# A two-layer hybrid attention trunk: polynomial logarithm, a fourth raw weight buffer, other copies for queries and keys, and a shifted order

## The chip, the core and the metric

The kernel runs on one core of a Trainium2 chip. The metric is the device time of one execution, in microseconds. A core has TensorE (PE, with its weight loads shown apart as PEld), VectorE (DVE), ScalarE (ACT), GpSimd (POOL) and SyncE (SP, which here only issues transfers). The profile shows each engine's instructions with the line of the source that issued them.

## The reference

A trunk of two layers on x of 256 x 1024. Each layer normalises x, projects it with one matrix to all that the mixers need, runs three causal mixers of eight heads of 64 (MoBA, DSA, FoX), multiplies each by its SiLU gate, projects each back, merges the three by sigmoid gates and adds the output projection to x:

```
h = rms_norm(x, gain);  proj = h @ w_in          # 1024 -> 9296 columns
oa = moba(rope(qa), rope(ka), va) * silu(ga)
ob = dsa(rope(qb), rope(kb), vb, rope(q_idx), rope(k_idx), w_idx) * silu(gb)
log_f = log_sigmoid(f_logit + f_bias)            # 256 x 8
oc = fox(qc, kc, vc, log_f) * silu(gc)           # logits += cumsum(log_f)[t] - cumsum(log_f)[s]
y = stack([oa, ob, oc]) @ w_branch               # 512 -> 1024 each
x = x + sum(sigmoid(merge) * y) @ w_out
```

With 256 tokens the MoBA mixer is plain causal attention. DSA scores all keys with eight index heads, `sum_h w[t,h] * relu(q_idx . k_idx)`, and each query keeps its 64 best.

## The kernel before

**Split products.** All matrix products are made from two parts of each operand, a high one (what is left of an fp32 number after rounding to the type fp32r) and a low one (the rest): high x high, low x high and high x low. So a weight piece is loaded into a `raw` buffer by SP, ACT writes its high part `wh` (L374), DVE writes `wl = raw - wh` (L378), and PE runs the 24 matmuls of a unit (L419, 128 x 256 results, into one of three PSUM banks `proj`). Six `wh` and six `wl` ring slots and three `raw` buffers are cycled.

**Units.** The projection goes in units of 128 columns: the index key (`kwf`, with the DSA weights and FoX logits beside it), four index queries, then for each mixer four pairs of heads with a query, a key and a gate unit, merge gates, and the units of w_branch and w_out. A unit's result is taken from PSUM by DVE and ACT.

- Rope (index, MoBA and DSA queries and keys): DVE shuffles rows into `rsh` (L468), POOL multiplies it (L469), DVE makes `rr` (L470), POOL adds them (L471). There are two buffers of each.
- `write_q` (a query): ACT writes the high part `qh` (L405 or, with a scale, L409) and DVE the low part `qy` (L406, L410). Since PE contracts over 128 rows and a head has 64, ACT then packs by three half-height copies (L591): `qx` gets head 0's high rows and its low rows, and `qy` head 1's high rows above its low ones.
- `write_bd` (a key): ACT copies the rows of each head into the high tile `bd..h` twice (L744 from the source, L746 from itself to the other half), four half-height copies, and DVE writes the low rows `bd..l` (L748).
- Scores: three matmuls (L604, L606 twice) for 128 queries, three for the other 128, into the two PSUM banks `s`.
- Index heads: ACT takes relu out of the two banks (L818, 256 columns; L819, 512 columns) into `tmp`, DVE adds it up, weighted, in `isc` (L827, L829). Then eight rounds of MAX and MATCH_REPLACE (L849, L850) find the 64 best.
- Attention: DVE adds the mask and takes row maxima (L665, into `e` and `st`), ACT exponentials (L669), DVE reciprocals (L673), ACT or DVE the normalisation (L677 or L680), PE transposes (L692) into the two PSUM banks `t`, ACT and DVE split the result (L695, L697), PE multiplies by the values (L708 to L711) into the one PSUM bank `o`.
- Logarithm of the forget gates: `fz` holds six small tiles of 128 x 16. ACT takes an exponential (L777) and Ln (L778), DVE corrects the result for small arguments in nine steps (L782 to L790), and PE forms the cumulative sum (L796, L797). An instruction `ACT_TABLE_LOAD` stands ahead of Ln (L778) and ahead of the first tanh after it (L863).
- Merge: the tanh of a gate goes to `acc` (L863) or `mth`; later DVE multiplies and adds the branches (L897, L899; POOL can do the add, L900).

**What sets the order.** The order of every engine is fixed ahead by a list scheduler in the program (`Plan.run`). Each operation has one or more engines, costs, the buffers it uses and a key, which is mostly the number of its unit. The scheduler goes through a model of the time; the engine that can start first takes, of the operations that could start by then, the one with the smallest key. A tile is given to an operation when one of its kind is free, so the number of buffers changes the order too.

Of the kernel before, what the change touches and what calls it, by code (L numbers as in the profile page):

```python
# [9 lines left out]
F32 = mybir.dt.float32  # L10
F32R = mybir.dt.float32r
AF = mybir.ActivationFunctionType
ALU = mybir.AluOpType

L = 2
S = 256
# [13 lines left out]
C_ID, C_UT, C_MASK, C_ROPE, C_END = 0, 128, 256, 512, 1024  # L30
SWAP = list(range(8, 16)) + list(range(0, 8)) + list(range(16, 32))

R_RING = 6
R_RAW = 3
# [17 lines left out]
def shape_constants():  # L52
# [18 lines left out]
    return c  # L71

# [23 lines left out]
class Plan:  # L96
# [8 lines left out]
    def op(self, ways, reads, writes, key, lag=0.0, name="", touch=()):  # L105
# [20 lines left out]
        o.n, o.out, o.need, o.end = len(self.ops), [], 0, None  # L126
        for d in o.deps:
            if d is not o:
                d.out.append(o)
                o.need += 1  # L130
# [113 lines left out]
def hybrid_trunk(ctx, tc, x, norm_gain, w_in, forget_bias, w_branch, w_out, final_gain, consts, out):  # L244
# [15 lines left out]
    def T(b):  # L260
        return b.slot[1]
# [83 lines left out]
    for nm, n, cols, dt in (("rsh", 2, S, F32), ("rr", 2, S, F32),  # L345
# [238 lines left out]
    def write_q(src, n_ps, key, scale=None, name="q"):  # L584
# [5 lines left out]
        for t, o, a, b, i in ((q[1], up, q[0], up, 0), (q[1], dn, q[2], up, 1), (q[2], up, q[0], dn, None)):  # L590
            act(lambda t=t, o=o, a=a, b=b: ACT.activation(T(t)[o], T(a)[b].bitcast(F32), AF.Copy), S, False, [a],  # L591
                [q[2]] if i is None else [kx[i]], key, name, touch=[t], half=True)
# [142 lines left out]
    def write_bd(src, b, toks, key, ps, shared=False):  # L735

        up, dn = slice(0, 64), slice(64, 128)
        for h, o in enumerate((up, dn)):
# [4 lines left out]
            if not (shared and h):  # L743
                act(lambda hi=hi, s=s: ACT.activation(hi(), s(), AF.Copy), S, ps, [src], [toks[g][0]], key, "bd", touch=[b], half=True)  # L744
# [5 lines left out]

# [7 lines left out]
    def wf_cols(l, key):  # L758
# [17 lines left out]
        def ln():  # L776
            ACT.activation(e, na, AF.Exp)  # L777
            ACT.activation(u, e, AF.Ln, bias=1.0)  # L778
        act(ln, 0, False, [], [k_lf], key, "ln", 1540.0)
        act(lambda: None, 0, False, [k_lf], [], key - 1, "table", 1190.0)  # L780

        for f in (lambda: DVE.tensor_scalar(c, e, 1.0, None, op0=ALU.add),  # L782
                  lambda: DVE.tensor_scalar(na, c, 1.0, None, op0=ALU.is_equal),
                  lambda: DVE.tensor_scalar(c, c, -1.0, 5e-8, op0=ALU.add, op1=ALU.max),
                  lambda: DVE.reciprocal(c, c),
                  lambda: DVE.tensor_tensor(c, c, e, op=ALU.mult),
                  lambda: DVE.tensor_tensor(u, u, c, op=ALU.mult),
                  lambda: DVE.tensor_tensor(na, na, e, op=ALU.mult),
# [328 lines left out]
```

## Time and profile before

| what | value |
|---|---|
| time, median of 3 runs (lowest to highest) | 618.05 us (617.97 to 618.89) |
| time of the profiled execution | 618.74 us |
| its span | 616.9 us |
| PE busy | 606.5 us (98%) |
| DVE busy | 534.5 us (87%) |
| ACT busy | 451.7 us (73%) |
| POOL busy | 95.0 us (15%) |
| granted PE clock, mean | 0.997 |
| moved by DMA | 107.32 MB, mean 174 GB/s |

The span runs from the first to the last thing that the profile shows; 618.74 - 616.9 = 1.84 us of the execution lie around it. A row of a timeline gives the start (us from the span's start), the duration, engine, line, operation and tiles, and in brackets how long the engine had been idle and who released it. Instructions of an engine overlap a little, so what one costs in a row of them is the distance from its start to the next one's. The chain of waits follows the end back to its causes and gives for each piece only the time that counts.

### The profile page before, as it was taken

To read this page: it belongs to the slowest core of one execution; us is meant where nothing else is said; L and a number is where in the kernel's file an instruction comes from. 1 tells how busy PE (TensorE), PEld (TensorE's weight loads), DVE (VectorE), ACT (ScalarE), POOL (GpSimd) and SP (SyncE) were. 2 spreads that over 40 slices of the span, in tenths; PEclk is the share of its full clock that TensorE was granted. 3 is DMA by queue.
4 is the path that set the end of the run, shared out by engine and by line. 5 is a ranking of instruction groups with operands and counts; after the bars stand their busy time and mean duration, and the time that the engine had idled before them with its cause. 6 is when DMAs were issued, how large, how long until landed. Compare 5 with 4: busy or idle time off the path is not lost.

```text
span 616.9 us, 12615 instructions
## 1 busy us (share of the span) xinstructions
PE 606.5 (98%) x4804; PEld 581.1 (94%) x4804; DVE 534.5 (87%) x1322; ACT 451.7 (73%) x948; POOL 95.0 (15%) x101
## 2 busy tenths in 40 slices
PE   8999999999999999999999999999999999999995
PEld 6899999999998999999889999998999989999985
DVE  7899999985998889988588999998678988999773
ACT  5788398876996778775587866997688766987541
POOL 1251242000000233200006305300000013220001
PEclk9999999999999999999999999999999999999998
DMA  8962765655554563575555639455637365453711
GB/s 283 304 195 90 226 171 191 200 171 172 171 173 136 180 197 99 175 237 173 158 170 174 204 114 276 141 170 185 209 103 231 112 201 157 155 169 122 257 35 69
DMA packets 96156, 107.32 MB, mean 174 GB/s; under 512 B 4576, under 2 KB 84832, under 8 KB 96096
## 3 DMA queue, kind: packets, MB, share of 16 engines
q1 hardware_dynamic: 95808, 106.13, 54.7%
q8 instruction: 37, 0.61, 0.4%
q10 hardware_dynamic: 288, 0.39, 0.2%
q14 instruction: 23, 0.19, 0.1%
HBM read 103.37 MB, written 1.05 MB: 169 GB/s over the span
## 4 chain that ended last, share of the span: by engine, by line
PE 78%; DVE 13%; ACT 4%; issue 2%; DMA 1%; POOL 1%; SPq 0%; POOLq 0%; DVEq 0%; ACTq 0%
PE proj L419 68%; DVE wl L378 5%; PE t L692 3%; DVE isc L850 2%; PE proj L996 1%; PE s L604 1%; PE s L606 1%; DVE t L849 1%; DMA x<-in_x_dram 1%; DVE isc L829 1%; DVE rsh L468 1%; ACT wh L374 1%; PE o L708 1%; PE o L711 1%; DVE rr L470 1%
## 5 line engine op out<-in xcount | busy, mean ns | idle before, releaser
L419 PE MATMUL proj<-hTh,wh 128*128 128x256 f32 (+1 forms) x1040 | 270.1, 278 | 0.0
L419 PE MATMUL proj<-hTl,wh 128*128 128x256 f32 (+1 forms) x1040 | 269.7, 277 | 0.0
L378 DVE TENSOR_TENSOR wl<-raw,wh 128x1024 fp32r<-128x1024 f32 (+1 forms) x190 | 235.5, 1248 | 38.3 <-ACT wh L374 37.7
L374 ACT ACTIVATE wh<-raw 128x1024 fp32r<-128x1024 f32 (+1 forms) x190 | 199.0, 1053 | 51.1 <-PE proj L419 41.3
L419 PE MATMUL proj<-hTh,wl 128*128 128x256 f32 (+1 forms) x1040 | 234.0, 278 | 0.0
L419 PEld LDWEIGHTS proj<-hTh,wh 128*128 128x128 f32 (+1 forms) x1040 | 194.7, 187 | 0.2
L419 PEld LDWEIGHTS proj<-hTl,wh 128*128 128x128 f32 (+1 forms) x1040 | 194.6, 187 | 0.3
L419 PEld LDWEIGHTS proj<-hTh,wl 128*128 128x128 f32 (+1 forms) x1040 | 175.6, 187 | 0.0
L469 POOL TENSOR_TENSOR rsh<-rsh,cst 128x256 f32<-128x256 f32 (+1 forms) x42 | 35.6, 849 | 351.9 <-DVE rsh L468 351.7
L471 POOL TENSOR_TENSOR rr<-rr,rsh 128x256 f32<-128x256 f32 (+1 forms) x42 | 51.1, 1220 | 8.2 <-DVE rr L470 5.4
L669 ACT ACTIVATE e<-e,st 128x128 f32<-128x128 f32 x96 | 42.7, 446 | 6.9 <-DVE st L665 6.6
L419 PE MATMUL proj<-wh,v 128*128 128x512 f32 (+1 forms) x144 | 35.5, 368 | 0.0
L419 PE MATMUL proj<-og0l,wh 128*128 128x256 f32 x128 | 33.9, 277 | 0.0
L419 PE MATMUL proj<-og0h,wh 128*128 128x256 f32 x128 | 32.4, 278 | 0.0
L419 PE MATMUL proj<-wh,hTh 128*128 128x512 f32 x80 | 32.4, 405 | 0.0
L419 PE MATMUL proj<-wh,hTl 128*128 128x512 f32 x80 | 31.5, 393 | 0.0
L419 PEld LDWEIGHTS proj<-wh,v 128*128 128x128 f32 x144 | 25.2, 188 | 4.7
L419 PE MATMUL proj<-og0h,wl 128*128 128x256 f32 x128 | 28.6, 277 | 0.0
L697 DVE TENSOR_TENSOR ptl<-t,pth 128x384 fp32r<-128x384 f32 x48 | 24.9, 551 | 0.6 <-ACT pth L695 0.6
L419 PE MATMUL proj<-wl,hTh 128*128 128x512 f32 x80 | 24.9, 392 | 0.0
L419 PEld LDWEIGHTS proj<-og0h,wh 128*128 128x128 f32 x128 | 24.0, 188 | 0.0
L419 PEld LDWEIGHTS proj<-og0l,wh 128*128 128x128 f32 x128 | 24.0, 188 | 0.0
(194 smaller groups left out, 1046.1 us busy)
## 6 DMA issues: line engine op xcount, KB each, us to landing
raw<-in_w_in_dram SPq DMA_DIRECT2D x74, 1024.0 KB, 5.3
raw<-in_w_branch_dram SPq DMA_DIRECT2D x24, 512.0 KB, 3.5
raw<-in_w_out_dram SPq DMA_DIRECT2D x8, 1024.0 KB, 6.9
tmp<-wf SPq DMA_DIRECT2D x16, 128.0 KB, 5.2
raw<-in_w_in_dram SPq DMA_DIRECT2D x3, 512.0 KB, 7.9
x<-in_x_dram SPq DMA_DIRECT2D x4, 256.0 KB, 5.1
raw<-in_w_in_dram SPq DMA_DIRECT2D x2, 320.0 KB, 6.0
out_dram<-tmp SPq DMA_DIRECT2D x2, 320.0 KB, 2.5
```

The source lines that it names most:

```text
L374: ACT.activation(p[0].v, sel(c.v), AF.Copy)
L378: DVE.tensor_tensor(p[1].v, sel(c.v), p[0].v.bitcast(F32), op=ALU.subtract)
L419: PE.matmul(o(), a(), b(), start=first and i == 0, stop=last and i == n - 1)
L468: dve(lambda: DVE.stream_shuffle(T(sh)[:np_], a(), SWAP), S, [ps], [sh], key, "rope")
L469: gps(lambda: POOL.tensor_tensor(T(sh)[:np_], T(sh)[:np_], s[:np_], op=ALU.mult), S, [k_rope], [sh], key, "rope")
L470: dve(lambda: DVE.tensor_tensor(T(r)[:np_], a(), c[:np_], op=ALU.mult), S, [ps, k_rope], [r], key, "rope")
L471: gps(lambda: POOL.tensor_tensor(T(r)[:np_], T(r)[:np_], T(sh)[:np_], op=ALU.add), S, [sh], [r], key, "rope")
L604: PE.matmul(o.rearrange("p (h c) -> p h c", h=2), qh[:, sl], kl[:, :, :n], start=True, stop=False)
L669: act(lambda t=t, a=a, n=n, e=e, st=st: ACT.activation(T(e)[:, a:a + n], T(e)[:, a:a + n], AF.Exp, bias=T(st)[:, t:t + 1], scale=-1.0, acc ...
L692: PE.transpose(T(ps)[:, i * 128:(i + 1) * 128], T(es[h])[:, i * 128:(i + 1) * 128], ident)
L697: dve(lambda h=h, src=src: DVE.tensor_tensor(T(pl)[:, h], src(), T(ph)[:, h].bitcast(F32), op=ALU.subtract), 384, [ps, kp[h][0]], [kp[h][1 ...
L850: dve(lambda o=o, t8=t8: DVE.match_replace(o, T(t8), o, TAKEN), n, [t8], [k_isc[i]], key + r * step, "top8")
```

## The change

It does four things.

1. The logarithm is computed without Ln. After the exponential e, DVE makes s = e / (2 + e) and sums an odd polynomial in s (`ATANH`), ten steps in place of nine. Ln and the operation "table" that was scheduled ahead of it are gone; so are the four `ACT_TABLE_LOAD` at L778 and L863.
2. There are four `raw` buffers for three, and four each of `rsh` and `rr` for two. The space comes from `dynamic_dma_scratch_size=1024`.
3. `write_q` makes `qx` by one full-height copy straight from the source, which puts head 0's high rows in place, and a half copy over its lower half; the copy into `qy` stays. `write_bd` of a key makes the high tile by one full-height copy of 512 columns and two half copies for four half copies. The index key (`shared`) keeps its copies.
4. A table `SHIFT` adds a number between -9 and 2 to the keys of 229 operations, by their running number.

The diff, with one line of the table:

```diff
-R_RAW = 3
+R_RAW = 4
...
+ATANH = (2.0, 0.666663146821, 0.400249102795, 0.279606027472, 0.281783350867)
...
+SHIFT = {
+    115: 1, 142: -6.5, 144: -0.5, 145: -7, 146: -1, 148: -3, 150: -5, 160: 2, 172: 2, 173: -6, 174: -1, 192: -4,
...
         o.n, o.out, o.need, o.end = len(self.ops), [], 0, None
+        o.key += SHIFT.get(o.n, 0.0)
...
-    for nm, n, cols, dt in (("rsh", 2, S, F32), ("rr", 2, S, F32),
+    for nm, n, cols, dt in (("rsh", 4, S, F32), ("rr", 4, S, F32),
...
-        for t, o, a, b, i in ((q[1], up, q[0], up, 0), (q[1], dn, q[2], up, 1), (q[2], up, q[0], dn, None)):
-            act(lambda t=t, o=o, a=a, b=b: ACT.activation(T(t)[o], T(a)[b].bitcast(F32), AF.Copy), S, False, [a],
-                [q[2]] if i is None else [kx[i]], key, name, touch=[t], half=True)
+        if scale is None:
+            act(lambda: ACT.activation(T(q[1]), src[0](), AF.Copy), S, n_ps, [src[1]], kx, key, name, touch=[q[1]])
+        else:
+            act(lambda: ACT.activation(T(q[1]), src[0](), AF.Copy, scale=scale), S, n_ps, [src[1]], kx, key, name, touch=[q[1]])
+        act(lambda: ACT.activation(T(q[1])[dn], T(q[2])[up].bitcast(F32), AF.Copy), S, False, [q[2]], [kx[1]], key, name,
+            touch=[q[1]], half=True)
+        act(lambda: ACT.activation(T(q[2])[up], T(q[0])[dn].bitcast(F32), AF.Copy), S, False, [q[0]], [q[2]], key, name, half=True)
...
+        if not shared:
+            act(lambda: ACT.activation(T(b)[0], T(src)[:, :S].unsqueeze(1).to_broadcast([128, 2, S]), AF.Copy), 2 * S, ps, [src],
+                [toks[0][0], toks[0][1], toks[1][0], toks[1][1]], key, "bd", touch=[b])
...
-                act(lambda hi=hi, s=s: ACT.activation(hi(), s(), AF.Copy), S, ps, [src], [toks[g][0]], key, "bd", touch=[b], half=True)
...
-        def ln():
-            ACT.activation(e, na, AF.Exp)
-            ACT.activation(u, e, AF.Ln, bias=1.0)
-        act(ln, 0, False, [], [k_lf], key, "ln", 1540.0)
-        act(lambda: None, 0, False, [k_lf], [], key - 1, "table", 1190.0)
+        act(lambda: ACT.activation(e, na, AF.Exp), 16, False, [], [k_lf], key, "lf")
+
+        s, s2, q = na, c, u
+        for f in (lambda: DVE.tensor_scalar(s2, e, 2.0, None, op0=ALU.add),
+                  lambda: DVE.reciprocal(s2, s2),
+                  lambda: DVE.tensor_tensor(s, e, s2, op=ALU.mult),
+                  lambda: DVE.tensor_tensor(s2, s, s, op=ALU.mult),
+                  lambda: DVE.tensor_scalar(q, s2, ATANH[4], ATANH[3], op0=ALU.mult, op1=ALU.add),
+                  lambda: DVE.tensor_tensor(q, q, s2, op=ALU.mult),
+                  lambda: DVE.scalar_tensor_tensor(q, q, ATANH[2], s2, op0=ALU.add, op1=ALU.mult),
+                  lambda: DVE.scalar_tensor_tensor(q, q, ATANH[1], s2, op0=ALU.add, op1=ALU.mult),
+                  lambda: DVE.scalar_tensor_tensor(q, q, ATANH[0], s, op0=ALU.add, op1=ALU.mult),
+                  lambda: DVE.scalar_tensor_tensor(lf, z, 0.0, q, op0=ALU.min, op1=ALU.subtract)):
...
-    nc = _bacc.Bacc("TRN2", target_bir_lowering=False, num_devices=1)
+    nc = _bacc.Bacc("TRN2", target_bir_lowering=False, num_devices=1, dynamic_dma_scratch_size=1024)
```

As the order counts instructions, PE stays at 4145 rows (a row can stand for several equal matmuls) with the same matmuls, and its projections keep their order: only the score, transpose, value and sum matmuls move among them. ACT goes from 846 instructions to 811, DVE from 1250 to 1260, POOL from 106 to 103 (four adds L899 to DVE, a gate product to POOL). On DVE there are also six normalisations more that ACT had before, and one less. The first rows that differ stand at about 28 us of the profile before on ACT and DVE and at about 40 us on PE; from about 575 us on the order of the three is the same again. After the change L374 is L401, L405 and L409 are L432 and L436, L406 and L410 are L433 and L437, L419 is L446, L468 is L495, L591 is L618 to L623, L665 is L696, L796 is L829, L818 and L819 are L851 and L852, L863 is L896.

The order at three places follows, at the second of them on two engines; the digits behind a name tell buffers apart, and they differ between the kernels.

ACT in the index stage of the first layer, before, from the large relu of one pair of index heads (L819, `tmp` from the second score bank) to the next one and past it:

```order
L819 ACTIVATE tmp_108<-s_163 128x512
L591 ACTIVATE qy_87<-qh_81 64x256
L591 ACTIVATE qx_85<-qh_82 64x256
L591 ACTIVATE qx_85<-qy_88 64x256
L591 ACTIVATE qx_83<-qh_80 64x256
L591 ACTIVATE qy_88<-qh_82 64x256
L591 ACTIVATE qx_83<-qy_86 64x256
L863 ACTIVATE acc<-proj_161 128x256
L374 ACTIVATE wh_67<-raw_120 128x1024
L818 ACTIVATE tmp_108<-s_162 128x256
L591 ACTIVATE qy_86<-qh_80 64x256
L819 ACTIVATE tmp_108<-s_163 128x512
```

The same place after, from the large relu (L852) to the next:

```order
L852 ACTIVATE tmp_108<-s_168 128x512
L896 ACTIVATE acc<-proj_166 128x256
L401 ACTIVATE wh_67<-raw_118 128x1024
L621 ACTIVATE qx_83<-qy_86 64x256
L851 ACTIVATE tmp_108<-s_167 128x256
L623 ACTIVATE qy_86<-qh_80 64x256
L852 ACTIVATE tmp_108<-s_168 128x512
```

Six half copies, of three index queries, stood ahead of acc and the weight split (L374) between the two relus, and one behind them; now one half copy stands behind acc and wh and one between the small and the large relu. The other copies of those queries are fewer, or stand ahead of the first relu.

DVE where the last steps of the logarithm (`fz`) are done in the first layer, before:

```order
L788 TENSOR_TENSOR fz<-fz 128x16
L849 MAX t_147<-isc 128x8
L789 TENSOR_TENSOR fz<-fz 128x16
L849 MAX t_148<-isc 128x8
L790 SCALAR_TENSOR_TENSOR fz<-fz 128x16
L850 MATCH_REPLACE isc<-t_147,isc 128x128
L850 MATCH_REPLACE isc<-t_148,isc 128x256
L633 SCALAR_TENSOR_TENSOR g_127<-th_125,proj_160 128x256
L378 TENSOR_TENSOR wl_75<-raw_118,wh_68 128x1024
L800 COPY csum<-t_165 128x16
L803 COPY wf<-t_165 128x256
L801 TENSOR_SCALAR ncs<-t_165 128x16
```

After:

```order
L819 TENSOR_TENSOR fz<-fz 128x16
L883 MATCH_REPLACE isc<-t_153,isc 128x256
L820 SCALAR_TENSOR_TENSOR fz<-fz 128x16
L405 TENSOR_TENSOR wl_70<-raw_119,wh_63 128x1024
L821 SCALAR_TENSOR_TENSOR fz<-fz 128x16
L405 TENSOR_TENSOR wl_71<-raw_120,wh_64 128x1024
L822 SCALAR_TENSOR_TENSOR fz<-fz 128x16
L664 SCALAR_TENSOR_TENSOR g_133<-th_131,proj_165 128x256
L823 SCALAR_TENSOR_TENSOR fz<-fz 128x16
L405 TENSOR_TENSOR wl_72<-raw_120,wh_65 128x1024
L882 MAX t_154<-isc 128x8
L833 COPY csum<-t_170 128x16
```

The steps on `fz` were set between the rounds of the search; now three `wl`, two gate products `g` and a search round more stand ahead of the last of them, and what reads the cumulative sum (csum) comes later by as much.

PE at that cumulative sum, before:

```order
L419 MATMUL proj_161<-hTh,wh_67 128x256
L419 MATMUL proj_161<-hTl,wh_67 128x256
L796 MATMUL t_165<-fz,cst 128x16
L797 MATMUL t_165<-fz,ones 128x8
L419 MATMUL proj_161<-hTh,wl_74 128x256
L419 MATMUL proj_161<-hTh,wh_67 128x256
```

After, with the six rows ahead of it:

```order
L446 MATMUL proj_164<-hTh,wh_68 128x256
L446 MATMUL proj_164<-hTh,wl_75 128x256 x2
L446 MATMUL proj_164<-hTl,wh_68 128x256
L446 MATMUL proj_164<-hTh,wl_75 128x256
L829 MATMUL t_170<-fz,cst 128x16
L830 MATMUL t_170<-fz,ones 128x8
L446 MATMUL proj_166<-hTh,wh_63 128x256
L446 MATMUL proj_166<-hTl,wh_63 128x256
```

The sum stood behind the first six matmuls of the unit in the third `proj` bank; now it stands behind 42 projection matmuls more, at the start of the unit after the next.

DVE at the row maxima of the first attention pair to be scored (`e` and `st` from the banks `s`), before, all four of them, with the low part of a query (`qy`) between:

```order
L378 TENSOR_TENSOR wl_72<-raw_119,wh_65 128x1024
L665 ISA e_131,st_135<-s_162,cst 128x128
L665 ISA st_135 128x1
L665 ISA e_131,st_135<-s_163,cst 128x256
L665 ISA st_135 128x1
L665 ISA e_132,st_136<-s_162,cst 128x128
L665 ISA st_136 128x1
L410 SCALAR_TENSOR_TENSOR qy_86<-rr_124,qh_80 128x256
L665 ISA e_132,st_136<-s_163,cst 128x256
L665 ISA st_136 128x1
L378 TENSOR_TENSOR wl_73<-raw_120,wh_66 128x1024
```

After:

```order
L437 SCALAR_TENSOR_TENSOR qy_86<-rr_127,qh_80 128x256
L495 STREAM_SHUFFLE rsh_124<-proj_165 128x256
L497 TENSOR_TENSOR rr_128<-proj_165,cst 128x256
L696 ISA e_136,st_140<-s_167,cst 128x128
L696 ISA st_140 128x1
L696 ISA e_137,st_141<-s_167,cst 128x128
L696 ISA st_141 128x1
L696 ISA e_136,st_140<-s_168,cst 128x256
L696 ISA st_140 128x1
L696 ISA e_137,st_141<-s_168,cst 128x256
L696 ISA st_141 128x1
L704 RECIPROCAL st_140<-st_140 128x1
```

The copy qy went from between the maxima to ahead of them, and the order of the four is now: both of the smaller bank, then both of the larger one.

More of the change, by code (lines that the diff above doesn't have):

```diff
@@ L71, in shape_constants @@
     return c
+SHIFT = {
[21 rows of a table added]
+}
 CUR = [""]
@@ L737, in write_bd @@
         up, dn = slice(0, 64), slice(64, 128)
+        if not shared:
+            act(lambda: ACT.activation(T(b)[0], T(src)[:, :S].unsqueeze(1).to_broadcast([128, 2, S]), AF.Copy), 2 * S, ps, [src],
+                [toks[0][0], toks[0][1], toks[1][0], toks[1][1]], key, "bd", touch=[b])
+        else:
+            act(lambda: ACT.activation(T(b)[0][up, 0], T(src)[up, :S], AF.Copy), S, ps, [src], [toks[0][0]], key, "bd", touch=[b],
+                half=True)
         for h, o in enumerate((up, dn)):
@@ L774, in wf_cols @@
         dve(pre, 0, [ps, k_fb], [k_lf], key, "lf", 300.0)
-        def ln():
-            ACT.activation(e, na, AF.Exp)
-            ACT.activation(u, e, AF.Ln, bias=1.0)
-        act(ln, 0, False, [], [k_lf], key, "ln", 1540.0)
-        act(lambda: None, 0, False, [k_lf], [], key - 1, "table", 1190.0)
[L782 to L788, printed above, removed]
-                  lambda: DVE.tensor_tensor(u, u, na, op=ALU.add),
-                  lambda: DVE.scalar_tensor_tensor(lf, z, 0.0, u, op0=ALU.min, op1=ALU.subtract)):
+        act(lambda: ACT.activation(e, na, AF.Exp), 16, False, [], [k_lf], key, "lf")
[10 more added lines that the diff above has]
+                  lambda: DVE.scalar_tensor_tensor(lf, z, 0.0, q, op0=ALU.min, op1=ALU.subtract)):
             dve(f, 0, [], [k_lf], key + 10, "lf", 100.0, port=True)
```

20 rows, old and new, of the table SHIFT are left out of this document.

## The prediction

> **What bounds the kernel now.** I read the page first. Its chain of work that ended last names the engine that sets the end:
>
> ```profile
> span 616.9 us, 12615 instructions
> ...
> PE 78%; DVE 13%; ACT 4%; issue 2%; DMA 1%; POOL 1%; SPq 0%; POOLq 0%; DVEq 0%; ACTq 0%
> ```
>
> The end hangs on PE for 78% of the span and on DVE for 13%. The order gives PE the same 4145 rows, with the same matmuls, before and after the change. So the time can fall only where PE stands still, and the second view is the waits of PE's weight loads, from 20 us to the end (columns: who waits, for whom, us in total, times, longest):
>
> ```profile
> PEld s L604 <- ACT tmp L819: 1.0, 3, 0.5
> PEld t L796 <- DVE fz L790: 0.8, 2, 0.6
> PEld t L692 <- ACT e L677: 0.3, 1, 0.3
> PEld o L708 <- ACT bd0h L744: 0.3, 1, 0.3
> PEld s L604 <- DVE st L665: 0.2, 1, 0.2
> ```
>
> These five rows are all that PE waits for after 20 us: eight waits, 1.0 + 0.8 + 0.3 + 0.3 + 0.2 = 2.6 us. Ahead of that, and in the last stage (from 575 us), the rows of PE, DVE and ACT stand in the same order in both kernels, so the waits there are taken as unchanged. **The most that this change can take out is about 2.6 us, 0.42% of the span.**
>
> Third, busy time by stage, to see who has room where these waits lie (first layer's index stage, its selection stage, and the second layer's selection stage; columns: stretch, its length, busy PE, PEld, DVE, ACT, POOL, then clock, DMA share, GB/s):
>
> ```profile
> 31.00:60.00 29.00, 28.63 (x246) 28.24 (x245) 26.91 (x71) 25.34 (x48) 10.65 (x11) 1.00 0.48 150
> 60.00:88.00 28.00, 27.91 (x240) 27.48 (x239) 27.88 (x86) 17.12 (x35) 9.91 (x8) 1.00 0.68 201
> 360.00:388.00 28.00, 27.54 (x237) 27.03 (x236) 27.88 (x86) 17.03 (x36) 8.99 (x8) 1.00 0.74 216
> ```
>
> ACT is busy 25.34 of 29 us in the index stage and has 11 us free in the selection stage, where DVE has nothing free: 27.88 of 28 us, in both layers.
>
> **Edit 1: the copies for queries and keys (ACT).** What a half-height copy takes, as a group of ACT's (x count: shortest/median/longest ns), and then two pieces of the chain of waits (start, us that count, what) for the next prices:
>
> ```profile
> L591 ACT ACTIVATE qx<-qh x32: 397/417/422, 36.5 to 541.8; 64x256 fp32r<-64x256 f32 x32
> ```
>
> ```profile
> 43.01 0.30 ACT qh L405
> 43.31 0.50 ACT tmp L819
> ```
>
> A query unit had three half-height copies, 3 x 0.42 = 1.26 us; it gets one full-height copy, priced by the qh row of the same size at 0.30, and two halves, 0.84: 1.14 us, so 0.12 saved, 32 times: 3.8 us. A key unit had four halves of the same 64x256, 1.68 us; it gets one full copy of 512 columns, by the 512-column relu 0.50, and two halves: 1.34, so 0.34 saved, 24 times: 8.2 us. That is 12 us. The trace of before has neither full copy in that place; if they took 0.42, as much as a half, and 0.57, as the longest relu below, the savings would be 0 and 0.27 x 24 = 6.5 us. ACT has room in each of the stages above, so nearly all of these 6.5 to 12 us lies beside PE's work and counts nothing. It counts where a half copy stands ahead of something PE waits for. That place is this, on ACT and then on PE:
>
> ```profile
> 46.48 0.38 ACT L863 ACTIVATE acc<-proj 128x256 f32<-128x256 f32 x1
> 46.76 1.05 ACT L374 ACTIVATE wh<-raw 128x1024 fp32r<-128x1024 f32 x1
> 47.71 0.37 ACT L818 ACTIVATE tmp<-s 128x256 f32<-128x256 f32 x1
> 48.11 0.41 ACT L591 ACTIVATE qy<-qh 64x256 fp32r<-64x256 f32 x1
> 48.43 0.57 ACT L819 ACTIVATE tmp<-s 128x512 f32<-128x512 f32 x1
> ```
>
> ```profile
> 49.06 0.50 PE L604 MATMUL s<-bd0l,qh 128*128 128x512 f32 x1 [0.37 <-ACT tmp L819]
> ```
>
> PE needs the second score bank, which relu L819 empties at 49.00; the one before it ended at 43.81 (43.31 + 0.50). Between them ACT ran six half copies, acc, wh, the small relu and another half copy: 5.2 us. In the new order only acc, wh, a half copy, the small relu and a half copy stand between the same two relus. By starts in these rows that is acc 0.28 (46.48 to 46.76), wh 0.95, half 0.44, small relu 0.40, half 0.32 and the relu's 0.57: 2.96 us. The bank comes free 2.2 us earlier, PE asks for it 0.5 us earlier than it got it, and in the new order that third score group also stands six projection matmuls (0.7 us) further up: about 1 us to spare. The same holds in the second layer. Taken: the 1.0 us of the first row goes, all of it. In the FoX units the full copy reads the projection's own bank, so 16 times a bank is read 0.30 us longer or less; no row of PE waits for a projection bank, so this counts zero (if that cover were gone: up to 16 x 0.30 = 4.8 us).
>
> **Edit 2: the logarithm.** The table loads, as the group at L778, and one of those at L863 with what follows it:
>
> ```profile
> L778 ACT ACT_TABLE_LOAD  x2: 1283/1283/1283, 28.8 to 327.9; - x2
> ```
>
> ```profile
> 40.11 1.28 ACT L863 ACT_TABLE_LOAD   x1
> 41.41 0.38 ACT L863 ACTIVATE acc<-proj 128x256 f32<-128x256 f32 x1
> ```
>
> The load at L778 and the one back at L863 stand once in each layer: 4 x 1.28 = 5.1 us of ACT go. The Trainium skill ("ScalarE: Activation LUTs", section "What ACT_TABLE_LOAD costs") adds a drain of about 1.38 us to each load, by which the four would be worth 10.6 us. The trace shows no such drain: the load from 40.11 to 41.39 is followed by acc at 41.41. Either way PE does not wait on these loads, so they count zero by themselves; their cover is the weights already split ahead. The ten polynomial steps on DVE replace nine, one more small step in each layer. What decides is when the last is done, for PE's cumulative sum (L796) waits for it. DVE there, first the chain of waits, with a stretch of 42 projection matmuls as PE's price, then the engine's own rows:
>
> ```profile
> 60.77 0.07 DVE fz L790
> 60.85 0.66 DVE isc L850 x3
> 61.50 0.33 DVE g L633
> 61.83 1.14 DVE wl L378
> ...
> 93.98 4.77 PE proj L419 x42
> ```
>
> ```profile
> 46.85 0.18 DVE L786 TENSOR_TENSOR fz<-fz 128x16 f32<-128x16 f32 x1
> 47.06 0.18 DVE L787 TENSOR_TENSOR fz<-fz 128x16 f32<-128x16 f32 x1
> 47.85 1.23 DVE L378 TENSOR_TENSOR wl<-raw,wh 128x1024 fp32r<-128x1024 f32 x1 [0.61 <-ACT wh L374]
> ```
>
> The order moves the cumulative sum behind 42 more projection matmuls: 4.77 us later. It also puts more of DVE's work ahead of the last log step: three wl (3 x 1.14), two g (2 x 0.33), one search pair (0.66) and one step net (0.07), together 4.8 us. The two shifts cancel; but PE now arrives earlier by the waits gone ahead of it: first layer 0.5 (score bank) + 0.2 (its own old wait) = 0.7 us, second layer 0.5 + 0.6 = 1.1 us. So if DVE is as idle as before, waits of 0.7 and 1.1 us stand there, 1.8 us where 0.8 stood. What DVE gets back: the six log steps that ran one behind the other at 0.21 us each (46.85 to 47.06) are now set between other work, where one costs 0.07 (60.77 to 60.85): some 6 x 0.14 = 0.8 us; and the 0.61 us that it stood idle for a wh which was queued behind half copies. That is up to 1.4 us in a layer, more than 1.1. Taken: 0.2 us in each layer, between 0 and the 1.8 for both. So 0.8 goes and 0.4 comes.
>
> **Edit 3: four raw buffers, four for the rope.** What ACT's weight split waits for, over the whole run (us, times):
>
> ```profile
>   PE proj L419: 41.3, 44
>   DMA raw<-in_w_in_dram: 6.1, 5
> ```
>
> The split waits 44 times for PE to give up a ring slot and five times, 6.1 us, for a load; no row of PE above waits for a weight. A raw buffer more lets loads start earlier into time that PE does not lack: taken at zero, with the split ring as cover. The smaller scratch for dynamic DMA touches no load here, as SP and ACT issue them all. The rope buffers matter by what they allow to overlap; that is the second rival.
>
> **Edit 4: the shifted order.** It takes the copy qy (L410) out from between the row maxima of the first attention pair:
>
> ```profile
> 85.44 0.41 DVE L410 SCALAR_TENSOR_TENSOR qy<-rr,qh 128x256 fp32r<-128x256 f32 x1
> 85.77 0.41 DVE L665 CUSTOM_DVE_ANT_0 e<-s,cst 128x256 f32<-128x256 f32 x1
> ```
>
> The copy costs 0.33 (start to start) and the last maximum ended at 86.18, just when PE wanted the bank. Without it the bank is free 0.33 us earlier, which covers the wait of 0.2. The other two single waits (0.3 and 0.3) are at places where the order also moved rows; they may go or move. Four adds of the merge (L899) go from POOL to DVE, at 0.33 by the copy's row, 1.3 us in all: zero, as no row of PE waits in the merge stage. Moved groups can also meet new waits. Before, six of the eight waits, 1.8 us, lay at the some hundred attention groups of PE, the other two at the sums. I take new ones at 0.4 us, a quarter of that; the bounds are 0 and 1.8.
>
> **The sum.** 2.6 out, 0.4 in at the cumulative sums, 0.4 in elsewhere: 1.8 us less. The profiled execution (618.74 us, its span 616.9 and 1.84 around it) would become 616.9, its span 615.1. The median of the three runs, 618.05, is 0.7 below that execution; the same 1.8 off it gives **616.3 us**. A measurement of this kernel can tell 0.2% (1.24 us) from no change: faster is under 616.8, slower above 619.3.
>
> **Rivals.** First, *the wait only moves* (no change, about 617.7). The cumulative sums wait the full 1.8 us and new waits elsewhere bring 0.4: 2.6 - 2.2 = 0.4 gained. For it: DVE is full in the selection stage, so lateness there is not made up. Against it: the DVE time that the log steps and the idle row give back lies ahead of the sum. It decides from 1.0 us of waits more than I took. Chance 0.27, with smaller gains of other kinds in it.
>
> Second, *DVE and POOL in each other's way* (slower, about 619.7). With four rope buffers POOL's rope steps may run beside other DVE work than now. What that does, on DVE and then POOL:
>
> ```profile
> 338.55 1.79 DVE L378 TENSOR_TENSOR wl<-raw,wh 128x1024 fp32r<-128x1024 f32 x1
> 340.26 0.96 DVE L406 TENSOR_TENSOR qy<-rr,qh 128x256 fp32r<-128x256 f32 x1
> 341.14 1.21 DVE L378 TENSOR_TENSOR wl<-raw,wh 128x1024 fp32r<-128x1024 f32 x1
> ```
>
> ```profile
> 339.33 1.60 POOL L471 TENSOR_TENSOR rr<-rr,rsh 128x256 f32<-128x256 f32 x1
> ```
>
> The wl that ran while POOL worked took 1.79 us, the next one, free of it, 1.21: 0.58 us a collision. In the selection stage DVE has 0.12 us of 28 free, so each added collision there is passed on to the score banks and transposes that PE waits for. From three more in each layer, 6 x 0.58 = 3.5 us against the 1.8 gained, the kernel is measurably slower: 618.05 + 1.7 = 619.7. The Trainium skill ("SBUF — State Buffer", section "Who interferes with whom") states that a DVE instruction with two SBUF inputs and a GpSimd instruction that reads SBUF exclude each other, the later one waiting for all of the earlier. By that rule such a meeting would cost up to the 1.60 us of the POOL step, and two in each layer would do. The rows side with half a block: both ran at once, both slower. Against this rival: the count of rope steps is unchanged, and such meetings are in the time of before already. Chance 0.13.
>
> That the change doesn't do what it says is hardly a rival: the order shows fewer ACT rows and moved PE rows.
>
> **How the numbers follow.** Forecast (gain of 1.24 us or more) 0.60, at 616.3; no change 0.27, about 617.7; slower 0.13, about 619.7. Low end: all 2.6 goes, nothing comes, and as much as 0.4 more is gained from small gaps that no row shows: 615.0. High end: past the 617.7 of the first rival by the 0.9 us that the spread of the three runs (617.97 to 618.89) puts on it: 618.6. That leaves out the slower rival and a little at the low end, under 2 in 10.
>
> **What would show it.** PE's load waits after 20 us should come to about 0.8 us; the score bank's row behind the relu should be gone, and so should ACT's table loads after the first exponential. Waits for the last log step of 0.5 us or more would be the first rival; wl rows with a higher mean in the selection stages, and PE waiting there on DVE, the second. I am wrong if PE's waits after 20 us are as long as before, or if the time fell by more than 3 us, which would mean that PE's own instructions or the stages that I held fixed had changed.

## The result and the profile after

The changed kernel takes 614.36 us (median of 4 runs, 614.34 to 614.57) against 618.03 before (4 runs, 617.97 to 618.89): a ratio of 0.9935 with the 95% interval 0.9919 to 0.9951. That is 3.7 us, where 1.8 were forecast, and 0.6 us below the range.

The page of the changed kernel, its span and the chain that ended last:

```profile
span 612.5 us, 12615 instructions
...
PE 96%; DVE 1%; issue 1%; DMA 0%; POOL 0%; ACT 0%; POOLq 0%; DVEq 0%
```

The end now hangs on PE for 96% of the span, before for 78%. The waits of PE's weight loads from 20 us to the end, of which there were five rows with eight waits and 2.6 us:

```profile
PEld t L829 <- DVE fz L823: 0.2, 1, 0.2
```

Busy time in the same three stretches as before:

```profile
31.00:60.00 29.00, 29.00 (x252) 28.82 (x251) 28.06 (x75) 24.30 (x48) 9.65 (x11) 1.00 0.48 155
60.00:88.00 28.00, 28.00 (x245) 27.91 (x244) 27.97 (x92) 19.98 (x46) 7.81 (x8) 1.00 0.68 209
360.00:388.00 28.00, 28.00 (x244) 27.75 (x244) 27.91 (x95) 19.15 (x41) 8.71 (x8) 1.00 0.82 253
```

PE has no idle time left in any of them. DVE was busy 1.15 us more in the index stage (28.06 for 26.91), so it stood idle less ahead of the selection stage, where it is as full as before.

ACT in the index stage, from one large relu (L852) to the next, answers to the seven copies between two relus before:

```profile
42.61 0.59 ACT L852 ACTIVATE tmp<-s 128x512 f32<-128x512 f32 x1
43.08 0.39 ACT L896 ACTIVATE acc<-proj 128x256 f32<-128x256 f32 x1
43.35 1.07 ACT L401 ACTIVATE wh<-raw 128x1024 fp32r<-128x1024 f32 x1
44.44 0.42 ACT L621 ACTIVATE qx<-qy 64x256 fp32r<-64x256 f32 x1
44.89 0.38 ACT L851 ACTIVATE tmp<-s 128x256 f32<-128x256 f32 x1
45.30 0.42 ACT L623 ACTIVATE qy<-qh 64x256 fp32r<-64x256 f32 x1
45.62 0.58 ACT L852 ACTIVATE tmp<-s 128x512 f32<-128x512 f32 x1
```

From the end of one relu (43.20) to the end of the next (46.20) are 3.0 us, by the forecast 2.96, before 5.2. PE takes that bank at 46.93, so 0.7 us are to spare where about 1 was forecast.

**One measure for all runs.** The 13th projection matmul starts at 13.27 us in the profile of before and at 12.45 in that of after. That head is not set by the change: it is 13.02 to 13.27 in the three profiles of the old program, and 12.27 to 13.16 in those of kernels with all or part of the change. So the profiles are compared from that matmul on: 616.94 - 13.27 = 603.7 us before, 612.54 - 12.45 = 600.1 after, 3.6 less. By this measure the three profiles of kernels that run the old program (before, experiments 1 and 5) agree to 0.1 us. The medians differ by 3.7, so hardly any of the gain lies in the head.

### The profile page after: what moved, and what is told of

It reads as the page before. It is cut to its first block, busy times and chain, and to the rows that moved or that the text cites. A ratio compares the mean times of both kernels' runs of the same rounds, so it can differ in the third digit from the quotient of the medians.

```text
span 612.5 us, 12615 instructions
## 1 busy us (share of the span) xinstructions
PE 603.7 (99%) x4804; PEld 580.1 (95%) x4804; DVE 536.5 (88%) x1332; ACT 437.1 (71%) x913; POOL 92.3 (15%) x98
## 4 chain that ended last, share of the span: by engine, by line
PE 96%; DVE 1%; issue 1%; DMA 0%; POOL 0%; ACT 0%; POOLq 0%; DVEq 0%
PE proj L446 84%; PE t L723 3%; PE s L637 2%; PE s L635 2%; PE proj L1029 1%; PE o L742 1%; PE o L739 1%; DMA x<-in_x_dram 0%; PE o L741 0%; PE o L740 0%; DVE wl L1021 0%; DVE hTl L561 0%; DVE wh L1019 0%; PE t L547 0%; DVE tmp L513 0%
## 5 line engine op out<-in xcount | busy, mean ns | idle before, releaser
L446 PE MATMUL proj<-hTh,wh 128*128 128x256 f32 (+1 forms) x1040 | 270.3, 278 | 0.0
L446 PE MATMUL proj<-hTl,wh 128*128 128x256 f32 (+1 forms) x1040 | 270.0, 277 | 0.0
L405 DVE TENSOR_TENSOR wl<-raw,wh 128x1024 fp32r<-128x1024 f32 (+1 forms) x190 | 231.6, 1228 | 30.7 <-ACT wh L401 29.3
L446 PE MATMUL proj<-hTh,wl 128*128 128x256 f32 (+1 forms) x1040 | 234.0, 278 | 0.0
L401 ACT ACTIVATE wh<-raw 128x1024 fp32r<-128x1024 f32 (+1 forms) x190 | 199.9, 1055 | 46.9 <-PE proj L446 44.0
L446 PEld LDWEIGHTS proj<-hTh,wh 128*128 128x128 f32 (+1 forms) x1040 | 194.7, 187 | 0.3
L446 PEld LDWEIGHTS proj<-hTl,wh 128*128 128x128 f32 (+1 forms) x1040 | 194.7, 187 | 0.3
L446 PEld LDWEIGHTS proj<-hTh,wl 128*128 128x128 f32 (+1 forms) x1040 | 175.7, 187 | 0.0
L700 ACT ACTIVATE e<-e,st 128x128 f32<-128x128 f32 (+1 forms) x96 | 42.8, 449 | 12.2 <-DVE st L696 11.7
L446 PE MATMUL proj<-wh,v 128*128 128x512 f32 (+1 forms) x144 | 35.5, 368 | 0.0
L446 PE MATMUL proj<-og0l,wh 128*128 128x256 f32 x128 | 33.8, 276 | 0.0
L446 PE MATMUL proj<-og0h,wh 128*128 128x256 f32 x128 | 32.3, 277 | 0.0
L446 PE MATMUL proj<-wh,hTh 128*128 128x512 f32 x80 | 32.1, 401 | 0.0
L446 PE MATMUL proj<-wh,hTl 128*128 128x512 f32 x80 | 31.3, 392 | 0.0
L446 PEld LDWEIGHTS proj<-wh,v 128*128 128x128 f32 x144 | 25.2, 188 | 4.7
L446 PE MATMUL proj<-og0h,wl 128*128 128x256 f32 x128 | 28.6, 276 | 0.0
L446 PE MATMUL proj<-wl,hTh 128*128 128x512 f32 x80 | 24.9, 392 | 0.0
L899 ACT ACTIVATE mth<-proj 128x256 f32<-128x256 f32 x32 | 12.2, 381 | 16.9 <-PE proj L446 16.8
L446 PEld LDWEIGHTS proj<-og0h,wh 128*128 128x128 f32 x128 | 24.0, 188 | 0.0
```

The lines of the kernel that those rows point to most:

```text
L401: ACT.activation(p[0].v, sel(c.v), AF.Copy)
L405: DVE.tensor_tensor(p[1].v, sel(c.v), p[0].v.bitcast(F32), op=ALU.subtract)
L446: PE.matmul(o(), a(), b(), start=first and i == 0, stop=last and i == n - 1)
L700: act(lambda t=t, a=a, n=n, e=e, st=st: ACT.activation(T(e)[:, a:a + n], T(e)[:, a:a + n], AF.Exp, bias=T(st)[:, t:t + 1], scale=-1.0, acc ...
L899: act(lambda: ACT.activation(T(th), T(ps)[:, :S], AF.Tanh, scale=0.5), S, True, [ps], [th], u - EARLY, "mth")
```

## The experiments

All runs, with the median of before taken beside each. "Shown" is the sum and number of PE's load waits after 20 us; "from 13th" the span less the start of the 13th projection matmul, in the one profile of each kernel.

| run | us | before | shown | from 13th |
|---|---|---|---|---|
| before | 618.03 | | 2.6, 8 | 603.7 |
| after | 614.36 | 618.03 | 0.2, 1 | 600.1 |
| 1 before again | 618.63 | 618.13 | 2.6, 8 | 603.7 |
| 2 no table | 617.05 | 618.13 | 2.2, 6 | 602.5 |
| 3 half copies in place | 615.57 | 618.13 | 1.0, 2 | 601.2 |
| 4 Ln in place | 616.23 | 618.13 | 1.6, 3 | 601.9 |
| 5 scratch only | 618.33 | 618.26 | 2.7, 8 | 603.7 |
| 6 old copies and Ln, new order | 617.43 | 618.26 | 2.4, 4 | 602.8 |
| 7 old buffers | 616.88 | 618.26 | 2.0, 4 | 602.6 |
| 8 table in first layer only | 615.55 | 618.26 | 1.1, 3 | 601.1 |
| 9 three raw buffers | 614.49 | 618.73 | 0.2, 1 | 600.0 |
| 10 two rope buffers | 616.92 | 618.73 | 2.0, 4 | 602.6 |
| 11 no table, old buffers | 617.60 | 618.73 | 2.9, 5 | 603.2 |
| 12 new work in old order | 616.01 | 618.73 | 1.8, 4 | 602.7 |

**1. Before, once more.** No edit.

> The kernel before, unchanged, profiled once more. Its profiled execution of before took 618.74 us against a median of 618.03, and in its trace PE reaches the 13th projection matmul at 13.27 us, 0.82 us later than in the trace of after (12.45), though nothing in that stretch was changed. Theory A: those 0.8 us are a difference between executions in the first 13 us; a second profile of the same kernel then has a span near 616.2 us, reaches that matmul near 12.5 us, and shows the same eight waits of PE after 20 us, 2.6 us in sum. Theory B: the change shortens the head; then this profile shows 13.2 to 13.3 us again and a span near 616.9.

The span was 616.9 us again, and the 13th projection matmul came at 13.20, against theory A for the head; the waits after 20 us and the time from that matmul on (603.7) were as expected. By itself this left the head open.

**2. The change without the table.**

```diff
-SHIFT = {
-    115: 1, 142: -6.5, ...
-}
+SHIFT = {}
```

> The changed kernel with an empty table SHIFT: logarithm, buffers and copies stay, and the order is what the scheduler makes of the unchanged keys. Theory A (the gain is PE's waits taken out place by place by the moved operations, and the shorter ACT work alone only moves waits about): 616.0 to 618.0 us, with 1.5 to 3 us of PE waits after 20 us in the profile, some at other places than before. Theory B (the shorter ACT work does it): 614.2 to 615.2 us.

617.05 us, 1.1 under before: theory A. The waits of PE's loads in that kernel (its lines are 22 lower than those of after):

```profile
PEld proj L424 <- DVE rr L475: 1.2, 2, 0.6
PEld t L701 <- DVE e L689: 0.4, 2, 0.2
PEld s L613 <- DVE st L674: 0.3, 1, 0.3
PEld o L717 <- issue: 0.3, 1, 0.3
```

The waits for the relu and for the last log step are gone, but DVE now lets PE wait for projection banks (rr), normalised rows (e) and row maxima (st); with one wait that the profile puts down to nothing (issue) they come to 2.2 us. The shorter ACT work without the table mostly moved the waits. That is the first rival's outcome, but not its place: it had put them at the cumulative sums.

**3. Half copies put back, order kept.** A full copy becomes one half for a query, two for a key; every engine's order stays.

```diff
-            act(lambda: ACT.activation(T(q[1]), src[0](), AF.Copy), S, n_ps, [src[1]], kx, key, name, touch=[q[1]])
+            act(lambda: ACT.activation(T(q[1])[up], src[0]()[up], AF.Copy), S, n_ps, [src[1]], kx, key, name, touch=[q[1]])
...
-            act(lambda: ACT.activation(T(b)[0], T(src)[:, :S].unsqueeze(1).to_broadcast([128, 2, S]), AF.Copy), 2 * S, ps, [src],
+            def two():
+                for g, x in enumerate((up, dn)):
+                    ACT.activation(T(b)[0][x, g], T(src)[x, :S], AF.Copy)
+            act(two, 2 * S, ps, [src],
...
```

> The changed kernel in its own order on every engine, but each full-height copy is made by half-height copies again: one half into qx for a query, two halves into the high key tile. ACT has as much copying to do as before the change, at the same places. Theory A (about 1 us to spare at the score bank): 0.14 us more per query and 0.34 per key ahead of what waits behind them, mostly inside the spare time: 614.4 to 615.2 us, PE waits after 20 us of 0.2 to 1 us. Theory B (the copies carry the gain): 616 us or more, with waits for the relu at the score bank of about 1 us again.

615.57 us, 1.2 more than after, between the two theories. The wait is not at the relu:

```profile
PEld s L635 <- DVE bd2l L787: 0.8, 1, 0.8
PEld t L832 <- DVE fz L826: 0.2, 1, 0.2
```

PE waits 0.8 us for the low part of a key tile, which DVE can write only when ACT has copied the high one. That it is a key fits what the copies take (last section): a query's full copy takes as long as the half that replaces it here, a key's saves about 0.2 us.

**4. Ln put back, order kept.** The result of Ln is overwritten unused.

```diff
-        act(lambda: ACT.activation(e, na, AF.Exp), 16, False, [], [k_lf], key, "lf")
+        def ln():
+            ACT.activation(e, na, AF.Exp)
+            ACT.activation(u, e, AF.Ln, bias=1.0)
+        act(ln, 16, False, [], [k_lf], key, "lf")
```

> The changed kernel in its own order, but ACT also takes Ln where before did, right behind the exponential, with the table load ahead of it and the one back later; the result is overwritten unused. Adds 4 x 1.28 us of loads and two small instructions, about 5.5 us of ACT. Theory A (the loads were covered): 614.4 to 614.9 us. Theory B (the loads held up PE in the index stage): 615.5 us or more, with PE waits for ACT in the stretch from 28 to 50 us or 325 to 350 us.

616.23 us, 1.9 more than after: theory B, and a clear miss for "the loads were covered".

```profile
PEld t L832 <- DVE fz L826: 0.9, 1, 0.9
PEld s L635 <- ACT tmp L855: 0.4, 1, 0.4
PEld s L635 <- ACT tmp L854: 0.3, 1, 0.3
```

The 5.5 us of ACT come back as waits for the relus and for the last log step. The row behind the load shows again no pause: the load ends at 40.91 and the next instruction starts at 40.92 (ACT, the same kernel):

```profile
39.63 1.28 ACT L899 ACT_TABLE_LOAD   x1
40.92 0.39 ACT L899 ACTIVATE acc<-proj 128x256 f32<-128x256 f32 x1
```

**5. The smaller scratch alone.**

```diff
-    nc = _bacc.Bacc("TRN2", target_bir_lowering=False, num_devices=1)
+    nc = _bacc.Bacc("TRN2", target_bir_lowering=False, num_devices=1, dynamic_dma_scratch_size=1024)
```

> The kernel before with dynamic_dma_scratch_size=1024 and nothing else; the order is the same on every engine, only the tiles lie at other addresses. Both profiles of before reach the 13th projection matmul at 13.20 to 13.27 us, all four of kernels with the change at 12.27 to 12.51. Theory A (the smaller scratch, and with it where the tiles lie, lets the first transfers run faster): that matmul near 12.4 us, and 617.3 to 617.8 us. Theory B (the fourth raw buffer does it): 13.2 us as before, and 618.0 to 618.3 us. From that matmul to the end 603.7 us as in both profiles of before, by either.

618.33 against 618.26: nothing, theory A fell. The 13th matmul came at 13.02. Experiment 7 had it at 12.49 with three raw buffers, experiment 9 at 12.99 with three and experiment 10 at 13.15 with four, so the fourth raw buffer doesn't set it either. What makes it vary was not found.

**6. All old ACT work in the new order.** Edits 3 and 4 together.

> The changed kernel in its own order on every engine, with both the half copies and Ln put back in place: the new order with all of ACT's old work. Put back one at a time they cost 1.2 us (615.57) and 1.9 us (616.23) against 614.36. Theory A (each part covers waits of its own): 3.1 us together, 617.3 to 617.7 us. Theory B (both lengthen the same waits in the index stage, and what is late once is not late twice): 616.3 to 616.9 us. If the order alone carried the gain it would stay under 615.5.

617.43 us: theory A. The waits of 3 and 4 stand there side by side:

```profile
PEld t L835 <- DVE fz L829: 0.9, 1, 0.9
PEld s L635 <- DVE bd2l L787: 0.8, 1, 0.8
PEld s L635 <- ACT tmp L858: 0.4, 1, 0.4
PEld s L635 <- ACT tmp L857: 0.3, 1, 0.3
```

**7. Old numbers of buffers, table kept.**

```diff
-R_RAW = 4
+R_RAW = 3
...
-(("rsh", 4, S, F32), ("rr", 4, S, F32),
+(("rsh", 2, S, F32), ("rr", 2, S, F32),
```

> The changed kernel with three raw buffers and two each for the rope, scratch and table as changed; the scheduler orders anew with fewer buffers. Theory A (PE never waits for a weight, so the buffers are worth nothing by themselves): 614.2 to 615.0 us. Theory B (the table fits the order that four buffers give, and with fewer the same shifts put operations elsewhere): 615.5 to 617.5 us with 1 us or more of PE waits after 20 us. The 13th projection matmul near 12.4 us if the scratch shortens the head, near 13.2 if the fourth raw buffer does.

616.88 us, 2.5 more than after: theory B. 9 and 10 tell which buffers.

**8. The table in the first layer only.** The second layer's operations begin at number 1580.

```diff
-        o.key += SHIFT.get(o.n, 0.0)
+        o.key += SHIFT.get(o.n, 0.0) if o.n < 1580 else 0.0
```

> The changed kernel with the table used for the operations of the first layer alone. Without the table the time was 617.05, with it 614.36: 2.7 us. Theory A (it removes single waits in each layer, independent of each other): the first layer keeps its part and the second looks as without the table; about half of 2.7 is lost, 615.4 to 616.1 us. Theory B (one layer carries it): 614.4 to 614.8 or 616.7 to 617.1 us.

615.55 us: theory A. To the 2061st projection matmul, in the first layer's output projection, this kernel takes 288.6 us from the 13th, as after does (288.7; without the table 290.1), and from there to the last projection matmul 305.9, as without the table (305.9; after 304.9). The waits that are left are all the second layer's own.

**9 and 10. One kind of buffer at a time.** The two lines of experiment 7, one each.

> The changed kernel with three raw buffers, rope buffers at four, table as changed; the scheduler orders anew. Both kinds of buffer taken back cost 2.5 us (616.88 against 614.36). Theory A (raw buffers decide, since they set when SP, ACT and DVE may take the next piece): 616.0 to 617.2 us, and the rope buffers alone under 615.4. Theory B (rope buffers decide): 614.3 to 615.2 us here. If the table fits nothing but the exact order of four and four, both single runs lose 1 us or more.

> The changed kernel with two buffers each for rsh and rr, raw buffers at four, table as changed. Theory A (raw decides): 614.3 to 615.4 us. Theory B (rope decides): 616.0 to 617.2 us. If any other number of buffers spoils the table's fit: 615.4 us or more in both single runs.

With three raw buffers 614.49 us, and from the 13th matmul on 600.0, as after: the fourth raw buffer is worth nothing. With two rope buffers 616.92, as with both kinds taken back: theory B. The waits with two rope buffers:

```profile
PEld s L635 <- DVE st L696: 0.8, 2, 0.4
PEld proj L446 <- ACT acc L896: 0.7, 1, 0.7
PEld s L635 <- ACT tmp L852: 0.5, 1, 0.5
```

None of them is at a rope step. The scheduler hands out buffers as it goes, so with fewer of them it sets another order, which the table was not made for; whether two could do with another table stays open.

**11. Neither table nor buffers.** The empty table of 2 and the edit of 7.

> The changed kernel without the table and with the old numbers of buffers: logarithm and copies alone, in the order that the scheduler gives them. With four buffers and no table it was 617.05. Theory A (the buffers are worth nothing by themselves, only the table uses them): 616.6 to 617.5 us. Theory B (they are worth their 2.5 us with or without the table): 618.5 us or more, slower than before.

617.60 against 617.05 with four buffers: just above theory A's range, far from B. From the 13th matmul on it is 603.2 against 602.5. So the buffers are worth 0.4 to 0.8 us without the table (0.4 by the lowest times, 0.55 by the medians, 0.8 by the profiles) and 2.5 with it.

**12. New work in the old order.** Every engine keeps the order of before. Ln is replaced by a plain copy, so the forget gates are not those of the reference.

```diff
+            o, b = (slice(0, 128), slice(0, 128)) if i == 0 else (o, b)
...
+                def first(hi=hi, s=s, h=h):
+                    if shared:
+                        ACT.activation(hi(), s(), AF.Copy)
+                    elif h == 0:
+                        ACT.activation(T(b)[0], T(src)[:, :S].unsqueeze(1).to_broadcast([128, 2, S]), AF.Copy)
...
-            ACT.activation(u, e, AF.Ln, bias=1.0)
+            ACT.activation(u, e, AF.Copy)
```

> The kernel before in its own order on every engine, with the copies cut in place as the change cuts them (a full-height copy for one half of a query, one of 512 columns for two halves of a key), and with a plain copy in place of Ln, so that the four table loads go; the values of the forget gates are then not those of the reference. It is the fourth corner: old order and old work 603.66 us from the 13th projection matmul to the end, new order with old work 602.76, new order with new work 600.09. Theory A (work and order each bring their own part): 603.66 - 2.67 = 601.0 from that matmul on, 615.4 us. Theory B (the old order leaves most of the shorter work unused): 602.3 to 603.2, 616.7 to 617.8 us; the waits for the relu at the score bank shrink, those for the last log step and the row maxima stay.

The profile gives 602.7 us from the 13th matmul on, as theory B had it. The time, 616.01 (six runs from 615.22 to 617.31, with before at 618.73 beside them), lies between the two theories. The waits of the profiled execution:

```profile
PEld s L605 <- DVE st L666: 1.3, 2, 0.8
PEld t L693 <- ACT e L678: 0.3, 1, 0.3
PEld t L802 <- DVE fz L796: 0.2, 1, 0.2
```

The relu's row is gone, as expected. The row of the maxima grew from 0.2 to 1.3 in its place, and the last log step is nearly in time, which was not expected.

But this profile is of an execution of 617.06 us, and four of the other five took 1.0 to 1.8 us less. The head can't make up for that: the profile has the 13th matmul at 12.58, the earliest in any profile is 12.27. For every other kernel with more than one run, the stretch from the 13th matmul on, that earliest head and the 1.8 to 1.9 us around the span add up to its lowest time within 0.4 us; here the lowest time is 1.5 us under the sum. So in its fast executions this kernel must take less than 602.7, down to some 601.2, and none of these was profiled. By the times neither theory is settled.

The corners, from the 13th matmul on: old order and old work 603.7, new order and old work 602.8 (with the new buffers and log steps), new order and new work 600.1; old order and new work 602.7 in its profile, down to 601.2 by its lowest time. Order alone brings 0.9 us and both 3.6. Work alone brings 1.0 in the profile and up to 2.5 in the fastest run. So between nearly nothing and 1.7 us of the gain comes only from the two together; which of these it is stays open.

## Why the prediction was wrong

The direction and the mechanism were right: PE's work is the same, and the time fell by what PE no longer waits. The size was off by half, by these steps.

**"The most that this change can take out is about 2.6 us".** This step failed. The waits shown fell by 2.4 us (2.6 to 0.2), the time from the 13th matmul on by 3.6. A wait costs PE more than its row shows. The third score group of the index stage, before (0.51 of a wait) and after (none), with the load of its fourth matmul ahead of each:

```profile
49.06 0.19 PEld L604 LDWEIGHTS s<-bd0l,qh 128*128 128x128 f32 x1 [0.51 <-ACT tmp L819]
...
48.14 0.38 PE L604 MATMUL s<-bd0l,qh 128*128 128x256 f32 x1
48.36 0.22 PE L606 MATMUL s<-bd0h,qx 128*128 128x128 f32 x1
48.42 0.27 PE L606 MATMUL s<-bd0h,qy 128*128 128x128 f32 x1
49.06 0.50 PE L604 MATMUL s<-bd0l,qh 128*128 128x512 f32 x1 [0.37 <-ACT tmp L819]
49.40 0.28 PE L606 MATMUL s<-bd0h,qx 128*128 128x256 f32 x1
49.52 0.28 PE L606 MATMUL s<-bd0h,qy 128*128 128x256 f32 x1
49.64 0.28 PE L419 MATMUL proj<-hTh,wh 128*128 128x256 f32 x1
```

```profile
46.87 0.19 PEld L635 LDWEIGHTS s<-bd0l,qh 128*128 128x128 f32 x1
...
46.65 0.28 PE L635 MATMUL s<-bd0l,qh 128*128 128x256 f32 x1
46.76 0.22 PE L637 MATMUL s<-bd0h,qx 128*128 128x128 f32 x1
46.82 0.28 PE L637 MATMUL s<-bd0h,qy 128*128 128x128 f32 x1
46.93 0.45 PE L635 MATMUL s<-bd0l,qh 128*128 128x512 f32 x1
47.22 0.28 PE L637 MATMUL s<-bd0h,qx 128*128 128x256 f32 x1
47.34 0.28 PE L637 MATMUL s<-bd0h,qy 128*128 128x256 f32 x1
47.46 0.28 PE L446 MATMUL proj<-hTh,wl 128*128 128x256 f32 x1
```

From its first matmul to the one that follows, the group took 49.64 - 48.14 = 1.50 us and now takes 0.81: 0.69 for a wait shown as 0.51. Two things stand beside the row. After the change the load starts ahead of its matmul (46.87 for 46.93); behind the wait both start at 49.06, and the next matmul comes 0.34 us later instead of 0.29. And the first matmul stood behind a wait that no row lists: its bank was emptied by the small relu (L818, 47.71 + 0.37 = 48.08), its load started only at 48.14, after 0.07 us of idle time, and the next matmul came 0.22 us later instead of 0.11. The views of waits list no idle time as short as that, so the five rows were not all that PE waited for. That the late load is what costs the time beside the row is read from these rows; no run tests it alone.

Over the kernel, the distances between neighbouring matmuls can be held against their median for the same two matmuls in all fourteen profiles. Around the eight waits before, they are 3.6 us longer in sum, where the rows show 2.6; each wait carries 0.07 to 0.22 us beside its row. Around the one wait after, they are 0.27 longer for 0.16 shown. So 3.3 of the 3.6 us are gone at these places, 0.9 of them beside the rows; the other 0.2 is spread over the span. The low end of the range had allowed 0.4 us for gaps that no row shows.

The table of runs says the same: time less the waits shown is 599.8 to 599.9 with one wait (after, experiment 9), 600.0 to 600.3 with two or three (3, 4, 8), 600.4 to 600.6 with four (6, 7, 10; in 12 it is 600.9, of which 0.3 lie behind the last projection matmul, for a reason not found) and 601.0 to 601.1 with eight (before, 1 and 5). With six and five (2 and 11) it is 600.3, so the number of waits is not all of it.

A fall of more than 3 us was set as a sign that PE's own instructions or the stages held fixed had changed. The fall came, but neither had changed: from the 13th to the 73rd projection matmul both kernels take 12.3 us, from the 4013th to the end 36.4, and PE's projection matmuls average 278 ns in both.

**New waits, 0.4 at the sums and 0.4 elsewhere.** They came to 0.2 in all. The last log step in the first layer now ends on DVE at 63.41, and PE takes the sum at 64.00:

```profile
63.24 0.17 DVE L823 SCALAR_TENSOR_TENSOR fz<-fz 128x16 f32<-128x16 f32 x1
```

```profile
64.00 0.29 PE L829 MATMUL t<-fz,cst 128*128 128x16 f32 x2
64.14 0.37 PE L830 MATMUL t<-fz,ones 128*128 128x8 f32 x2
```

With DVE as idle as before the step would have ended 60.85 - 13.27 + 4.8 = 52.4 us after the 13th projection matmul; it ended 63.24 + 0.17 - 12.45 = 51.0 us after it. So DVE got 1.4 us back, all that was counted on at most: the sum waits 0.2 us in the second layer and not at all in the first. In sum, of the 1.8 us that the stretch from the 13th matmul on fell further than forecast, 0.9 are what the waits cost beside their rows, 0.2 lie elsewhere, and 0.6 are new waits that did not come.

**"Counted zero": copies and table loads.** The sum for the copies at the score bank was right (3.0 us between the relus). The price of the copies elsewhere was not: it set the duration of a half (0.42) against the distance of a full copy to the next row (0.30). By durations a query's full copy takes 0.38 to 0.41 us and saves next to nothing, a key's takes 0.60 to 0.63 for two halves of 0.38 to 0.41 each, and all copies together went from 80.5 to 75.7 us: 4.8 saved, where 6.5 to 12 were given. That the copies are hidden elsewhere, and that the loads "count zero by themselves", failed in the new order: put back, they cost 1.2 and 1.9 us. Cover was judged by the waits of the old order. What the loads alone cost there was not measured; copies and Ln together are worth 1.0 us there in the profile of experiment 12, and more by its times.

**Buffers at zero.** Right for the raw buffers (experiment 9). Wrong for the rope buffers, which I weighed only as a danger: without them the same table loses 2.5 us.

**The first rival** (the wait only moves) is near to what the profiles show of the shorter work alone: the change without the table gained 1.1 us, and the new work in the old order 1.0 in its profile, with other waits in place of the old ones (more in its faster executions, whose waits are not known). **The second** did not happen: the full-size wl, 1252 ns on average before, are 1232 after:

```profile
L405 DVE TENSOR_TENSOR wl<-raw,wh 128x1024 fp32r<-128x1024 f32 x188 | 230.1, 1232 | 30.7 <-ACT wh L401 29.3
```

The rows that the prediction shows for it don't clearly "side with half a block", either. The wl ended at 338.55 + 1.79 = 340.34, POOL's step beside it at 340.93 and qy at 341.22: 0.59 and 0.29 us after the one ahead, no more than each takes alone (0.73 the shortest of POOL's steps, 0.41 for qy). That is as if each had waited for most of the one ahead, and the price of 0.58 leaves out the 0.55 that qy lost. No run tests this.

## What to carry to other kernels

Where one engine does the same work before and after, its lost time is better read from the distance between instructions that both kernels have than from the wait rows, which here showed two thirds of it. Work taken off an engine that is not the bound and an order that uses the room should be costed together: the shorter work in the scheduler's own order gained 1.2 us, the shifted order with the old work 0.9, both 3.6. Whether a cost is "covered" has to be tried in the order that is to run: 5.5 us of ACT that were counted at zero cost 1.9 there. And one profile stands for a kernel only if its other runs agree with it, which those of experiment 12 don't.

## What the runs showed of the hardware

A copy over half the partitions takes as long as over all of them: 64x256 at 0.42 us against 128x256 at 0.41 in the changed kernel. What saves time is an instruction less: a key's one copy of 512 columns takes 0.62 us in place of two halves of 0.41 each, while a query's full copy in place of one half saves nothing.

```profile
L621 ACT ACTIVATE qx<-qy 64x256 fp32r<-64x256 f32 x32 | 12.6, 413 | 1.1 <-DVE qy L437 0.5
...
L620 ACT ACTIVATE qx<-rr 128x256 fp32r<-128x256 f32 x16 | 6.5, 407 | 0.0
...
L770 ACT ACTIVATE bd1h<-rr 128x512 fp32r<-128x512 f32 x6 | 3.7, 624 | 0.0
```

The time at which the first weights are there varied by 1.0 us between fourteen profiles (13th projection matmul at 12.27 to 13.27 us), by 0.25 between the three of the old program, while everything behind it repeated to 0.1 us in the three profiles of the old program. Experiment 12, whose runs differ by more than the head was seen to, suggests that this is not so for every kernel.
